# The SSD half of a layer's output projection, emitted between the last GLA heads

## The chip, the cores and the metric

The kernel runs on one core of a Trainium2 chip. The metric is the device time of one execution in microseconds (us). Five engines run side by side, each in the order that its own queue holds: PE (TensorE, matmuls, with PEld for its weight loads), DVE (VectorE), ACT (ScalarE), POOL (GpSimd) and SP (SyncE, which issues most of the weight loads). They wait for each other through semaphores.

## The reference

Two layers of a token mixer with an MLP after each, over 256 latent tokens and 256 context tokens of 1024 channels. The change lies in layer 0. There an SSD scan and a GLA scan (8 heads) run on one input projection, and one output projection takes both halves of their result:

```python
def finish(y, x, z, o, r):
    y = (y + d_skip[:, None] * x).reshape(bn, t, SSD_INNER) * silu(z)
    y = rmsnorm(y.reshape(bn, t, SSD_GROUPS, -1), ...).reshape(bn, t, SSD_INNER)
    o = rmsnorm(o, gla_norm_w).reshape(bn, t, GLA_VAL) * silu(r)
    return concatenate([y, o], axis=-1) @ w_out
...
x = x + g1l * ol          # g1: a gate out of the modulation, silu(c) @ ada_w + ada_b
x = x + g2l * sq_relu_mlp(modulate(rmsnorm(x, norm2_w), sh2l, sc2l), ...)
```

The first 1024 rows of `w_out` meet the SSD half `y`, the other 1024 the GLA half `o`. The gate `g1`, and `sh2`, `sc2`, `g2` for the MLP, come from a matrix product of their own, the modulation.

## The kernel before

Tokens of both kinds make one block of 512. Each fp32 weight tile is loaded by SP into a `wraw` buffer (4 of 512 KB, `RAW`), split by ACT (`whi`) and DVE (`wlo`) into two fp32r parts (`wtile` and `wsplit`, L211 to L225), and each product is three matmuls (`mm3`). An output tile of 128 channels over 1024 input channels is 24 matmuls of 512 columns into one of four PSUM banks called `psd`; small products and transposes go to four banks called `pss`.

The stretch around the change, in the order in which `emit` writes it:

- Left over from the input projection is the SSD gate: `z_proj` (L1242), four groups of two weight tiles and a last step that scales `xtm`, the SSD half with tokens on partitions, by its norm factor (four DVE operations of 128x1024 for `ssqz`). A generator `fill` hands these out; `ZN` says how many steps each turn of the loop takes.
- GLA runs by pairs of heads, t_ = 0 to 3 (called pair 0 to 3 here). `gla_in` (L1268) projects queries and keys (48 matmuls), multiplies the gates (`dlr,gw`), and has for each of the two directions a chain through ACT and DVE (`lin_elem`, L1108: gate, running sum, `ke`, `qt`, `kt`); PE then transposes `ke` and forms the chunk states (`su`, `g0st`, `g1st`). `gla_out` (L1301) makes, for each of the two heads, scores (`qt,kt` matmuls of 64 columns), masks and sums them on DVE (`pm`, `pa`), forms the output on PE (`vtm,pa` and `st,qt`), and normalises it on ACT and DVE into `vtm`. `gla_in` of the next pair is emitted ahead of `gla_out` of this one.
- The modulation is a generator `ad` of two groups (`ada_steps`, L227): each has 8 steps of two raw 512 KB loads and 4 matmuls (line L237; no split), then a copy and 4 transposes. `ADN` says how many steps run in each turn; the first group holds `g1`.
- Then the output projection: for the SSD half (`xtm`) and then the GLA half (`vtm`), 32 transposes turn it to channels on partitions (into `hhi` and `hlo`, or `mgh` and `mgl`), and each of its 8 tiles ends in two gated residual adds on DVE (`add_out`) into the residual stream. The residual stream waits in DRAM (`xd`) and is read back by a 2 MB load that ACT issues as soon as `xtm`, whose space it takes, has been turned.

The order on each engine isn't that of the text: a scheduler of the framework builds the queues from the emitted order, the buffers and its own estimate of times. The queues named below are what it made.

Of the kernel before, what the change touches and what calls it, by code (L numbers as in the profile page):

```python
# [10 lines left out]
F32R = mybir.dt.float32r  # L11
# [3 lines left out]
MUL, ADD, SUB, MIN, MAX = ALU.mult, ALU.add, ALU.subtract, ALU.min, ALU.max  # L15
PSUM = bass.MemoryType.PSUM

P = 128
T = 512
# [10 lines left out]
DTM = 11  # L30
NF = 4
AR = 12
ZN = 3, 1, 2, 2
ADN = 0, 6, 11, 0
WA = 0, 1
QP = -2, 1, 2, 5
VP = -2, -1, 0, -1
GP = -1, 0, 4, 6
# [3 lines left out]
def emit(tc, A, out):  # L42
    nc = tc.nc
    V, S, G, PE, Q = nc.vector, nc.scalar, nc.gpsimd, nc.tensor, nc.sync
    top = ExitStack()

    def pool(name, bufs=1, side=None, stack=top, space=None):
        kw = dict(name=name, bufs=bufs, reuse_waits="tile")
        if side:
            kw["side"] = side  # L50
        if space is not None:
            kw["space"] = space
        return stack.enter_context(tc.tile_pool(**kw))

    cp = pool("const")
    hp = pool("acts")
# [4 lines left out]
    def tl(p, shape, tag, dt=F32, bufs=None):  # L61
        kw = dict(tag=tag, name=tag)
        if bufs is not None:
            kw["bufs"] = bufs
        return p.tile(list(shape), dt, **kw)

    def ps_d():
        return tl(pd, [P, T], "psd")
# [26 lines left out]
    def stt(eng, o, a, s, b, op0, op1):  # L95
        eng.scalar_tensor_tensor(out=o, in0=a, scalar=s, in1=b, op0=op0, op1=op1)  # L96
# [48 lines left out]
    mod = [tl(cp, [P, 48, 2], f"mod{l}") for l in range(2)]  # L145
# [62 lines left out]
    lo_eng = [V]  # L208
    lo_n = [0]

    def wtile(W, k0, kt, c0, n):  # L211

        raw = tl(wp, [P, kt, n], "wraw", bufs=RAW)
        Q.dma_start(out=raw, in_=W[k0 * P:(k0 + kt) * P, c0:c0 + n].rearrange("(k p) c -> p k c", p=P))
        return wsplit(raw, kt, n)
# [44 lines left out]
    def step(it, n=1):  # L260
        for _ in range(n):
            next(it, None)

    def drain(it):
        for _ in it:
            pass
# [8 lines left out]
    HALF = {1: slice(0, 256), 0: slice(256, 512)}  # L275
# [47 lines left out]
    def gemm_f(ps, w, xs, first=True, last=True):  # L323

        n_ = len(xs)
        for k, x in enumerate(xs):
            mm3(ps, (w[0][:, k], w[1][:, k]), x, first and k == 0, last and k == n_ - 1)
# [11 lines left out]
    def ktiles(x, a=slice(None)):  # L339
        return [(x[0][:, k, a], x[1][:, k, a]) for k in range(x[0].shape[1])]  # L340
# [14 lines left out]
    xd = tc.dram_tile([8, P, T], F32, name="xd")  # L355
# [397 lines left out]
    xT = tl(pool("x0", stack=x0, side="right"), [P, 8, T], "xT0")  # L753
# [11 lines left out]
    for k in range(8):  # L765
        ps = ps_s()
# [12 lines left out]
    for k0, nk in ((0, 4), (4, 2), (6, 2)):  # L779
        ps = ps_s()  # L780
        ks, n = slice(k0, k0 + nk), nk * P
# [21 lines left out]
        src = p2[:, :nb * P].rearrange("p (b j h r) -> p j h b r", b=nb, j=2, h=2)[:, :, :, :, 0:2]  # L803
# [11 lines left out]
        for i, m in enumerate(order[:NF]):  # L815
# [3 lines left out]
            for kk in range(k0, k0 + nk):  # L819
                w = [w_[:, kk % 2, c_] for w_ in wq[(kk - k0) // 2]]  # L820
                mm3(first[m], w, (h[0][:, kk], h[1][:, kk]), kk == 0, kk == 7)
        for k in range(k0, k0 + nk):
            ps = ps_s()
# [9 lines left out]
    xp = pool("x", stack=lx)  # L833
    xtm = tl(xp, [P, 4, DM], "xtm")
    lay = ExitStack()
    l0 = pool("l0", stack=lay)
    vtm = tl(l0, [P, 4, DM], "vtm")
# [23 lines left out]
    for m in order:  # L861
        if m in first:
            ps = first[m]
        else:
            w = wtile(W0, 0, 8, 1024 + P * m, P)
            ps = ps_d()
            gemm_f(ps, w, ktiles(h))
        src = tl(cvp, [P, T], "cvs")
# [16 lines left out]
        if m < 4:  # L885
            k = 2 * m
# [47 lines left out]
    ps = ps_s()  # L934
# [5 lines left out]
    ps = ps_s()  # L940
# [109 lines left out]
    scr = [lambda: tl(s2, [P, T], "y", bufs=2)]  # L1050
    adn = [0]
# [6 lines left out]
    ad = counted(ada_all(lambda: scr[0](), (0, 1), (0, 2)))  # L1058
# [15 lines left out]
    fill = v_r_proj()  # L1074
# [157 lines left out]
    gla = ExitStack()  # L1232
# [30 lines left out]
    fill = vr_z()  # L1263

    def gla_w(t_):
        return [wtile(W0, 0, 8, c0 + P * t_, P) for c0 in (3104, 3616)]

    def gla_in(t_, ws):  # L1268
        qk = []
        for w, sc in zip(ws, (0.125, 1.0)):  # L1270
            ps = ps_d()
            gemm_f(ps, w, ktiles(h))
            d_ = tl(g2, [P, T], "gq" if sc != 1.0 else "gk", bufs=QB)
            act(d_, ps, AF.Copy, scale=sc)
            qk.append(d_)

        def chain(d):
            ps = ps_s()
            b0 = 64 + 32 * d
            mm(ps, gw[b0:b0 + 16, t_ * P:(t_ + 1) * P], dlr[b0:b0 + 16])  # L1280
            gb = vB[:, 24 + 4 * d + t_:25 + 4 * d + t_]
            e1 = tl(g2, [P, T], "ge1", bufs=2)
            act(e1, ps, AF.Abs, bias=gb)
            yield
            act(e1, e1, AF.Exp, scale=-1.0)
            yield
            act(e1, e1, AF.Ln, bias=1.0)
            lg = tl(g2, [P, T], "gc", bufs=2)
            ts(V, lg, ps, gb, ADD, 0.0, MIN)
            yield  # L1290
            tt(V, lg, lg, e1, SUB)
            yield
            nm = f"g{d}"
            qt, kt, kd, el, em = yield from lin_elem(g2, d, lg, qk[0], qk[1], None, 1.0 / 16.0, 0, nm)
            sts = yield from lin_states(g2, d, kd, el, em, lambda c, hh: vtm[:, c, (2 * t_ + hh) * P:(2 * t_ + hh + 1) * P],
                                        2, 0, nm)
            return qt, kt, sts

        return both([chain(d) for d in range(2)])

    def gla_out(t_, el_):  # L1301
        for hh in range(2):
            units = []
            r = slice(64 * hh, 64 * hh + 64)
            hd_ = 2 * t_ + hh
            hs_ = slice(hd_ * P, (hd_ + 1) * P)
            for c in range(4):
                cs_ = slice(c * P, (c + 1) * P)
                un = [(r, el_[0][1], el_[0][0], c * P), (r, el_[1][1], el_[1][0], c * P), vtm[:, c, hs_]]
                for d in range(2):  # L1310
                    s_ = el_[d][2].get(c)
                    un.append(None if s_ is None else (el_[d][0][r, cs_], s_[r]))
                units.append(un)

            def put(o, hs_=hs_, hd_=hd_):
                o3 = o.rearrange("p (c f) -> p c f", c=4)
                ov = vtm[:, :, hs_]
                sq = tl(g2, [P, 4, P], "pa", bufs=2)
                for c in range(4):
                    S.activation(out=sq[:, c], in_=o3[:, c], func=AF.Square, accum_out=osq[:, c, hd_:hd_ + 1])  # L1320
                tt(V, ov, o3, sr[:, :, hs_], MUL)
                rstd_small(osq[:, :, hd_:hd_ + 1], 128)
                tt(V, ov, ov, osq[:, :, hd_:hd_ + 1].to_broadcast([P, 4, P]), MUL)

            lin_out(g2, pmask, units, put)

    scr[0] = lambda: tl(g2, [P, T], "ge1", bufs=2)
    cur = gla_in(0, gla_w(0))
    wn = gla_w(1)
    for t_ in range(4):  # L1330
        step(fill, ZN[t_])
        nxt = gla_in(t_ + 1, wn) if t_ < 3 else None
        wn = gla_w(t_ + 2) if t_ < 2 else None
        step(ad, ADN[t_])
        if t_ == 3:
            drain(fill)
            step(ad, max(0, 10 - adn[0]))
        gla_out(t_, cur)
        cur = nxt
    gla.close()  # L1340


    lo_eng[:] = [V]
    WO = A["ssd_gla_w_out"][0]
    mgs = ExitStack()
    mg = pool("mixg", stack=mgs, side="right")
    scr[0] = lambda: tl(mg, [P, T], "adasb")
    for part, src in enumerate((xtm, vtm)):
        if part == 0:
            mx = [tl(hp, [P, 8, T], n, F32R) for n in ("hhi", "hlo")]  # L1350
        else:
            mx = [tl(mg, [P, 8, T], n, F32R) for n in ("mgh", "mgl")]
        for f in range(8):
            ps = ps_s()
            for c in range(4):
                tr(ps[:, c * P:(c + 1) * P], src[:, c, f * P:(f + 1) * P])
            nw = vB[:, 16 + f:17 + f] if part == 0 else vB[:, 96:97]
            act(mx[0][:, f], ps, AF.Copy, scale=nw)
            stt(V, mx[1][:, f], ps, nw, mx[0][:, f], MUL, SUB)
        if part == 0:  # L1360
            xT = tl(xp, [P, 8, T], "xtm")
            S.dma_start(out=xT, in_=xd.rearrange("k p t -> p k t"))
        def add_out(m):
            def put(s, ps):
                a = HALF[s]
                stt(V, xT[:, m, a], ps[:, a], mod[0][:, 16 + m, s:s + 1], xT[:, m, a], MUL, ADD)
            return put

        nf = 8 if part == 0 else 4
        for m in range(nf):  # L1370
            step(ad, WA[part])
            w = wtile(WO, 8 * part, 8, m * P, P)
            ps = ps_d()
            gemm_f(ps, w, ktiles(mx))
            for s in (1, 0):
                add_out(m)(s, ps)
    drain(ad)
    np_ = ExitStack()
    n1 = pool("norm", stack=np_)
# [102 lines left out]
    vtm = tl(l1, [P, 4, DM], "vtm")  # L1482
# [115 lines left out]
    cur = hgrn_in(0)  # L1598
    WO = A["hgrn_s5_w_out"][0]
    for hd_ in range(8):  # L1600
        projs(hd_)
        nxt = hgrn_in(hd_ + 1) if hd_ < 7 else None
# [6 lines left out]
        cur = nxt  # L1609
# [113 lines left out]
```

## Time and profile before

| | us |
|---|---|
| median of 3 runs (lowest, highest) | 1479.78 (1475.62, 1483.78) |
| the profiled execution | 1482.16 |
| its span, first to last instruction | 1480.4 |
| mean granted clock of TensorE in it | 0.973 |

[...] A busy PE isn't PE at its peak. In the chain of work that ended last each step is followed back to what released it. In a timeline row the bracket tells how long the engine sat idle before the row, and for whom.

### The profile page before, as it was taken

The page shows a single profiled execution, that of the slowest core. Times are in us where ns is not written, and L with a number is a line of the kernel's source. Part 1 is how long each engine was busy: PE and PEld are TensorE (multiplying, and loading weights), DVE is VectorE, ACT ScalarE, POOL GpSimd, SP SyncE. Part 2 cuts the span into 40 slices and gives each one's busy share as a digit, 9 for nine tenths or more (in the row PEclk, how much of TensorE's full clock was granted, in tenths as well). Part 3 has the DMA queues.
Part 4 walks back from the last instruction along what each step waited for, and adds up shares of the span by engine and source line. Part 5 has one row for each costly group of instructions (what it writes and reads, how often), then busy time and mean ns, then how long its engine had stood idle before and what let it go on. Part 6 is the DMA issues. An engine that isn't in the chain of part 4 may idle for free.

```text
span 1480.4 us, 24457 instructions
## 1 busy us (share of the span) xinstructions
PE 1426.6 (96%) x9662; PEld 1222.3 (83%) x9662; DVE 942.2 (64%) x1596; ACT 688.3 (46%) x1316; POOL 303.0 (20%) x340
## 2 busy tenths in 40 slices
PE   6999999999979999999999999999999999899998
PEld 4788998878746889877777777799988888899998
DVE  4698678876753455854563743374886988655543
ACT  5565545375532234531322422353286786555532
POOL 3000000000000003098077861122500000044210
PEclk9999999999985999999999999999999999999999
DMA  9733444421275433466467656649835332566762
GB/s 333 185 92 85 126 122 118 125 58 58 86 240 160 138 103 105 121 179 197 143 187 218 192 169 186 192 165 202 194 114 157 103 106 66 157 186 170 206 179 86
DMA packets 291151, 222.45 MB, mean 150 GB/s; under 512 B 22902, under 2 KB 270124, under 8 KB 291036
## 3 DMA queue, kind: packets, MB, share of 16 engines
q1 hardware_dynamic: 252752, 182.75, 42.5%
q0 software_dynamic: 6144, 22.05, 4.9%
q10 hardware_dynamic: 32140, 16.09, 4.4%
q8 instruction: 76, 1.25, 0.4%
q14 instruction: 39, 0.32, 0.1%
HBM read 206.39 MB, written 14.46 MB: 149 GB/s over the span
## 4 chain that ended last, share of the span: by engine, by line
PE 78%; DVE 8%; DMA 8%; ACT 4%; issue 2%; ACTq 0%; SPq 0%; DVEq 0%
PE psd L99 65%; PE pss L99 6%; DMA R<-acd 3%; PE pss L237 3%; PE pss L107 2%; DMA araw<-in_ada_w_dram 2%; DVE wlo L87 1%; DMA wraw<-in_ada_w_dram 1%; ACT hL L80 1%; DVE xtm L87 1%; ACT whi L80 1%; PE pss L652 1%; DMA U<-ud 0%; DMA ud<-s5r 0%; ACT R L80 0%
## 5 line engine op out<-in xcount | busy, mean ns | idle before, releaser
L87 DVE TENSOR_TENSOR wlo<-wraw,whi 128x1024 fp32r<-128x1024 f32 (+1 forms) x250 | 323.6, 1298 | 206.7 <-ACT whi L80 205.0
L80 ACT ACTIVATE whi<-wraw 128x1024 fp32r<-128x1024 f32 (+1 forms) x250 | 260.6, 1045 | 351.7 <-DMA wraw<-in_mlp_w_dram 170.7
L99 PE MATMUL psd<-hlo,whi 128*128 128x512 f32 (+1 forms) x1112 | 381.6, 345 | 1.3 <-DVE hlo L87 1.3
L99 PE MATMUL psd<-hhi,whi 128*128 128x512 f32 (+1 forms) x1112 | 378.5, 348 | 3.6 <-ACT hhi L80 3.6
L99 PE MATMUL psd<-hhi,wlo 128*128 128x512 f32 (+1 forms) x1112 | 380.8, 344 | 0.6 <-DVE wlo L87 0.6
L99 PEld LDWEIGHTS psd<-hhi,whi 128*128 128x128 f32 x1112 | 209.5, 191 | 36.0 <-ACT hhi L80 4.2
L99 PEld LDWEIGHTS psd<-hlo,whi 128*128 128x128 f32 x1112 | 211.3, 190 | 25.2 <-DVE hlo L87 2.3
L99 PEld LDWEIGHTS psd<-hhi,wlo 128*128 128x128 f32 x1112 | 211.3, 190 | 25.1 <-DVE wlo L87 1.0
L99 PE MATMUL psd<-wlo,hhi 128*128 128x256 f32 x576 | 165.5, 288 | 2.8 <-DVE wlo L87 2.8
L99 PE MATMUL psd<-whi,hlo 128*128 128x256 f32 x576 | 164.8, 286 | 0.0
L99 PE MATMUL psd<-whi,hhi 128*128 128x256 f32 x576 | 164.4, 287 | 0.0
L99 PEld LDWEIGHTS psd<-wlo,hhi 128*128 128x128 f32 x576 | 111.1, 193 | 4.7 <-DVE wlo L87 3.0
L99 PEld LDWEIGHTS psd<-whi,hhi 128*128 128x128 f32 x576 | 110.8, 193 | 2.7 <-issue 1.3
L99 PEld LDWEIGHTS psd<-whi,hlo 128*128 128x128 f32 x576 | 111.1, 193 | 0.6 <-issue 0.2
L99 PE MATMUL psd<-hidh,whi 128*128 128x512 f32 (+1 forms) x288 | 107.7, 375 | 0.0
L99 PE MATMUL psd<-hidl,whi 128*128 128x512 f32 (+1 forms) x288 | 105.6, 367 | 0.0
L99 PE MATMUL psd<-hidh,wlo 128*128 128x512 f32 (+1 forms) x288 | 105.5, 366 | 0.0
L87 POOL TENSOR_TENSOR nsa<-nsa,nsq 128x256 f32<-128x256 f32 x28 | 26.1, 934 | 370.1 <-ACT nsq L80 369.8
L96 DVE SCALAR_TENSOR_TENSOR xtm<-psd,mod,xtm 128x256 f32<-128x256 f32 x96 | 42.2, 476 | 66.6 <-PE psd L99 59.2
L99 PE MATMUL psd<-hl,whi 128*128 128x256 f32 x256 | 72.9, 285 | 0.0
L99 PE MATMUL psd<-hh,wlo 128*128 128x256 f32 x256 | 72.9, 285 | 0.0
L99 PE MATMUL psd<-hh,whi 128*128 128x256 f32 x256 | 72.4, 283 | 0.0
(448 smaller groups left out, 2447.4 us busy)
## 6 DMA issues: line engine op xcount, KB each, us to landing
wraw<-in_mlp_w_dram SPq DMA_DIRECT2D x128, 512.0 KB, 4.2
wraw<-in_ada_w_dram SPq DMA_DIRECT2D x80, 512.0 KB, 3.8
wraw<-in_ssd_gla_w_in_dram SPq DMA_DIRECT2D x48, 512.0 KB, 4.2
wraw<-in_hgrn_s_w_in_dram SPq DMA_DIRECT2D x43, 512.0 KB, 4.2
araw<-in_ada_w_dram SPq DMA_DIRECT2D x32, 256.0 KB, 7.8
R<-acd ACTq DMA_DIRECT2D x32, 256.0 KB, 3.9
wraw<-in_ssd_gla_w_out_dram SPq DMA_DIRECT2D x16, 512.0 KB, 4.6
wraw<-in_hgrn_s_w_out_dram SPq DMA_DIRECT2D x12, 384.0 KB, 3.4
```

The source lines that it names most:

```text
L80: ins = S.activation(out=out_, in_=in_, func=func, scale=scale, bias=bias)
L87: eng.tensor_tensor(out=o, in0=a, in1=b, op=op)
L96: eng.scalar_tensor_tensor(out=o, in0=a, scalar=s, in1=b, op0=op0, op1=op1)
L99: PE.matmul(o, lhsT=l, rhs=r, start=start, stop=stop, skip_group_check=True)
L107: PE.transpose(o, i, ident[:rows, :rows])
L237: ins = PE.matmul(ps[32 * gg:32 * gg + 32], lhsT=cs[:, k], rhs=raws[gg // 2][:, gg % 2 * T:gg % 2 * T + T], start=(k == 0), stop=(k == 7), ...
L652: PE.matmul(ps[64 * t2:64 * t2 + 64, 64 * a:64 * a + 64], lhsT=W1[i][:, a0 + a, 64 * t2:64 * t2 + 64], rhs=U[:, 2 * (a0 + a) + t2], start= ...
```

## The change

The SSD half of the output projection becomes a generator `ssd_out` that is emitted inside the loop over pairs: its 32 turns and 4 tiles behind the heads of pair 2, the other 4 tiles behind those of pair 3 (`SN`). One step of the modulation goes beside each of its 8 tiles (`step(ad)`), where before 17 steps ran in the loop's turns 1 and 2 (`ADN` 0, 6, 11, 0) and the last three beside the GLA half. Gate groups of `z_proj` go one turn later (`ZN` 3, 1, 2, 2 becomes 2, 1, 1, 1), and the rest of `fill` is drained in turn 2, not 3. The GLA half stays behind the loop.

```diff
-ZN = 3, 1, 2, 2
-ADN = 0, 6, 11, 0
-WA = 0, 1
+ZN = 2, 1, 1, 1
+ADN = 0, 6, 4, 0
+SN = 0, 0, 5, 4
...
+    def out_tile(mx, part, m):
+        w = wtile(WO, 8 * part, 8, m * P, P)
+        ps = ps_d()
+        gemm_f(ps, w, ktiles(mx))
+        for s in (1, 0):
+            add_out(m)(s, ps)
+
+    def ssd_out():
+        mx = [tl(hp, [P, 8, T], n, F32R) for n in ("hhi", "hlo")]
+        turned_mix(mx, xtm, 0)
+        res["x"] = tl(xp, [P, 8, T], "xtm")
+        S.dma_start(out=res["x"], in_=xd.rearrange("k p t -> p k t"))
+        yield
+        for m in range(8):
+            step(ad)
+            out_tile(mx, 0, m)
+            yield
...
+    so = ssd_out()
     for t_ in range(4):
         step(fill, ZN[t_])
         nxt = gla_in(t_ + 1, wn) if t_ < 3 else None
         wn = gla_w(t_ + 2) if t_ < 2 else None
         step(ad, ADN[t_])
-        if t_ == 3:
+        if t_ == 2:
             drain(fill)
-            step(ad, max(0, 10 - adn[0]))
+            step(ad, 10 - adn[0])
         gla_out(t_, cur)
+        step(so, SN[t_])
         cur = nxt
```

What the scheduler makes of it, at three places. First PE, where the keys of pair 2 are transposed (`ident,ke`), behind the gates of that pair (`dlr,gw`). Before, the gates of pair 2 are followed by 48 projection matmuls (`psd`):

```order
L99 MATMUL psd<-hhi,wlo 128x512
L99 MATMUL pss<-dlr,gw 128x512 x2
L99 MATMUL psd<-hhi,whi 128x512
L99 MATMUL psd<-hlo,whi 128x512
...
L99 MATMUL psd<-hhi,wlo 128x512
L107 MATMUL pss<-ident,ke 128x128 x6
L99 MATMUL pss<-vtm,g0kd 64x128 x2
```

After, the same gates stand inside the output of the heads of pair 0:

```order
L99 MATMUL pss<-vtm,pa 128x128
L99 MATMUL pss<-dlr,gw 128x512 x2
L99 MATMUL pss<-vtm,pa 128x128
L99 MATMUL pss<-g0st_3058,g0qt 128x128
L99 MATMUL pss<-vtm,pa 128x128
L99 MATMUL pss<-g0st_3072,g0qt 128x128
L99 MATMUL pss<-g1st_3093,g1qt 128x128
L99 MATMUL pss<-vtm,pa 128x128
L99 MATMUL pss<-g0st_3086,g0qt 128x128
L99 MATMUL pss<-g1st_3079,g1qt 128x128
L99 MATMUL pss<-vtm,pa 128x128
L107 MATMUL pss<-ident,ke 128x128 x6
```

Between gates and keys there are now nine small matmuls, the output of one head, in place of 48 projection matmuls.

Second DVE, where `xtm` is scaled (`xtm,ssqz`). Before, this stands ahead of the chain of pair 2 (`gc` is its gate), while PE has projection matmuls:

```order
L87 TENSOR_TENSOR vtm<-pss,sr 128x4x128
L87 TENSOR_TENSOR xtm<-xtm,ssqz 128x1024 x3
L87 TENSOR_TENSOR vtm<-vtm,osq 128x4x128
L87 TENSOR_TENSOR xtm<-xtm,ssqz 128x1024
L93 TENSOR_SCALAR gc<-pss,vB 128x512 x2
```

After, it stands behind the chain of pair 3 and ahead of that pair's states (`su`) and the masks (`pm`) of the heads of pair 2:

```order
L87 TENSOR_TENSOR ke<-ke,gk 128x384
L87 TENSOR_TENSOR ke<-ke,gk 128x512
L87 TENSOR_TENSOR g0kt<-gk,g0kt 128x512
L87 TENSOR_TENSOR g1kt<-gk,g1kt 128x512
L87 TENSOR_TENSOR xtm<-xtm,ssqz 128x1024 x4
L96 SCALAR_TENSOR_TENSOR su<-su,el,pss 128x128
L87 TENSOR_TENSOR wlo<-wraw,whi 128x1024
L96 SCALAR_TENSOR_TENSOR su<-su,el,pss 128x128
L87 TENSOR_TENSOR mod_88<-pss,vA 128x16 x2
L96 SCALAR_TENSOR_TENSOR su<-su,el,pss 128x128 x2
L1192 COPY_PREDICATED pm_2917<-mf,pss 64x512
```

The states, the modulation's bias add and the masks have moved behind the four scalings. Third DVE, at the heads of pair 3. Before, their masks follow those of pair 2, with no residual add between:

```order
L1196 COPY_PREDICATED pm_2918<-mb,pss 64x512
L87 TENSOR_TENSOR pa<-pm_2917,pm_2918 128x512
L87 TENSOR_TENSOR vtm<-pss,sr 128x4x128
L87 TENSOR_TENSOR vtm<-vtm,osq 128x4x128
L1192 COPY_PREDICATED pm_2917<-mf,pss 64x512
```

After, the residual adds of the first SSD tile (`xtm<-psd,mod,xtm`, which need the 2 MB load) stand ahead of the masked sum `pa` of pair 3's first head:

```order
L1196 COPY_PREDICATED pm_2918<-mb,pss 64x512
L96 SCALAR_TENSOR_TENSOR xtm<-psd,mod_88,xtm 128x256 x2
L87 TENSOR_TENSOR pa<-pm_2917,pm_2918 128x512
L1192 COPY_PREDICATED pm_2917<-mf,pss 64x512
L1193 COPY_PREDICATED pm_2917<-mf,pss 64x4x64
L1195 COPY_PREDICATED pm_2918<-mb,pss 64x4x64
L1196 COPY_PREDICATED pm_2918<-mb,pss 64x512
L87 TENSOR_TENSOR wlo<-wraw,whi 128x1024
L87 TENSOR_TENSOR pa<-pm_2917,pm_2918 128x512
```

That load and the split of the second SSD tile (`wlo`) are now on the way of pair 3's heads. On SP, 30 modulation loads in a row and then 8 of `w_out` have become 12, two of the last gate group, 6, and from there one `w_out` load and two modulation loads by turns.

## Rows read from the trace of the kernel before

**Rows 1.** The page, parts 1 and 4: busy time by engine; shares of the chain.

```profile
PE 1426.6 (96%) x9662; PEld 1222.3 (83%) x9662; DVE 942.2 (64%) x1596; ACT 688.3 (46%) x1316; POOL 303.0 (20%) x340
...
PE 78%; DVE 8%; DMA 8%; ACT 4%; issue 2%; ACTq 0%; SPq 0%; DVEq 0%
```

**Rows 2.** Windows: stretch, length, busy us (PE, PEld, DVE, ACT, POOL), PEclk, DMA share, GB/s.

```profile
396.00:423.00 27.00, 22.15 (x191) 12.24 (x191) 18.42 (x32) 12.70 (x42) 0.00 (x0) 1.00 0.64 214
423.00:441.00 18.00, 13.02 (x124) 6.16 (x116) 9.96 (x19) 5.97 (x16) 0.00 (x0) 0.80 0.77 262
441.00:488.00 47.00, 47.00 (x209) 30.97 (x206) 17.86 (x25) 11.31 (x45) 0.00 (x0) 0.50 0.52 158
```

**Rows 3.** Waits of PE from 285 to 565 us: total, times, longest.

```profile
PE pss L237 <- DMA wraw<-in_ada_w_dram: 8.2, 5, 3.2
PE psd L99 <- DVE wlo L87: 2.8, 1, 2.8
```

**Rows 4.** Timeline of PE, pair 1: start, us, operation; scores, output, modulation step.

```profile
406.01 1.09 PE L99 MATMUL pss<-g1qt,g1kt 64*64 64x64 f32 x16
407.03 0.49 PE L99 MATMUL pss<-vtm,pa 128*128 128x128 f32 x2
...
410.81 1.06 PE L237 MATMUL pss<-wraw,cs 128*32 128x512 f32 x8
```

**Rows 5.** Timeline of PE, pair 2: the same three; then the first SSD tile.

```profile
441.28 1.97 PE L99 MATMUL pss<-g1qt,g1kt 64*64 64x64 f32 x16
443.19 0.79 PE L99 MATMUL pss<-vtm,pa 128*128 128x128 f32 x2
...
449.83 1.93 PE L237 MATMUL pss<-wraw,cs 128*32 128x512 f32 x8
...
484.84 2.05 PE L99 MATMUL psd<-hhi,whi 128*128 128x512 f32 x4
```

**Rows 6.** Timeline of PE: pair 2's gates, first projection matmul, keys; a modulation step.

```profile
383.47 1.13 PE L99 MATMUL pss<-dlr,gw 16*128 16x512 f32 x4
384.53 0.50 PE L99 MATMUL psd<-hhi,whi 128*128 128x512 f32 x1
...
395.55 0.49 PE L107 MATMUL pss<-ident,ke 128*128 128x128 f32 x3
...
422.53 1.06 PE L237 MATMUL pss<-wraw,cs 128*32 128x512 f32 x8 [3.20 <-DMA wraw<-in_ada_w_dram]
```

**Rows 7.** Timeline of DVE: first step of pair 2's chain, last of each direction's keys.

```profile
386.82 1.40 DVE L93 TENSOR_SCALAR gc<-pss,vB 128x512 f32<-128x512 f32 x2
...
393.85 0.55 DVE L87 TENSOR_TENSOR ke<-ke,gk 128x384 f32<-128x384 f32 x1
...
395.52 0.68 DVE L87 TENSOR_TENSOR ke<-ke,gk 128x512 f32<-128x512 f32 x1
```

**Rows 8.** Groups of DVE from 380 to 490 us: count, busy us, mean ns, idle before.

```profile
L87 DVE TENSOR_TENSOR vtm<-pss,sr 128x512 f32<-128x512 f32 x7 | 4.8, 691 | 8.3 <-ACT pa L1320 8.2
L87 DVE TENSOR_TENSOR wlo<-wraw,whi 128x1024 fp32r<-128x1024 f32 x4 | 4.8, 1221 | 0.2 <-ACT whi L80 0.2
...
L87 DVE TENSOR_TENSOR xtm<-xtm,ssqz 128x1024 f32<-128x1024 f32 x4 | 4.7, 1217 | 0.0
```

**Rows 9.** DMA issues: count, KB each, median us from issue to landing.

```profile
wraw<-in_ada_w_dram SPq DMA_DIRECT2D x80, 512.0 KB, 3.8
...
xtm<-xd ACTq DMA_DIRECT2D x1, 2048.0 KB, 8.9
```

**Rows 10.** Windows, as in rows 2, where the clock came back.

```profile
428.00:430.00 2.00, 2.00 (x11) 0.80 (x7) 0.17 (x1) 1.31 (x3) 0.00 (x0) 0.50 0.34 72
430.00:432.00 2.00, 1.30 (x23) 1.08 (x21) 1.47 (x3) 1.94 (x7) 0.00 (x0) 0.92 0.95 334
...
486.00:488.00 2.00, 2.00 (x10) 1.70 (x9) 0.69 (x1) 0.88 (x6) 0.00 (x0) 0.50 0.02 6
488.00:490.00 2.00, 2.00 (x11) 1.70 (x10) 1.50 (x3) 1.26 (x3) 0.00 (x0) 0.91 0.00 0
```

More of the change, by code (lines that the diff above doesn't have):

```diff
@@ L1327, in emit, with turned_mix @@
     scr[0] = lambda: tl(g2, [P, T], "ge1", bufs=2)
[L1328 to L1334, printed above, removed]
-        if t_ == 3:
-            drain(fill)
-            step(ad, max(0, 10 - adn[0]))
[L1338 to L1343, printed above, removed]
-    WO = A["ssd_gla_w_out"][0]
[L1345 to L1352, printed above, removed]
+    WO = A["ssd_gla_w_out"][0]
+    res = {}
+    def turned_mix(mx, src, part):
         for f in range(8):
@@ L1359, in emit, with add_out, put @@
             stt(V, mx[1][:, f], ps, nw, mx[0][:, f], MUL, SUB)
[L1360 to L1376, printed above, removed]
+    def add_out(m):
+        def put(s, ps):
+            a = HALF[s]
+            x_ = res["x"][:, m, a]
+            stt(V, x_, ps[:, a], mod[0][:, 16 + m, s:s + 1], x_, MUL, ADD)
+        return put
+    def out_tile(mx, part, m):
[14 more added lines that the diff above has]
+            yield
+    cur = gla_in(0, gla_w(0))
+    wn = gla_w(1)
+    so = ssd_out()
+    for t_ in range(4):
+        step(fill, ZN[t_])
+        nxt = gla_in(t_ + 1, wn) if t_ < 3 else None
+        wn = gla_w(t_ + 2) if t_ < 2 else None
+        step(ad, ADN[t_])
+        if t_ == 2:
+            drain(fill)
+            step(ad, 10 - adn[0])
+        gla_out(t_, cur)
+        step(so, SN[t_])
+        cur = nxt
+    gla.close()
+    lo_eng[:] = [V]
+    mgs = ExitStack()
+    mg = pool("mixg", stack=mgs, side="right")
+    scr[0] = lambda: tl(mg, [P, T], "adasb")
+    mx = [tl(mg, [P, 8, T], n, F32R) for n in ("mgh", "mgl")]
+    turned_mix(mx, vtm, 1)
+    xT = res["x"]
+    for m in range(4):
+        step(ad)
+        out_tile(mx, 1, m)
     drain(ad)
```

## The prediction

> **What bounds the kernel now.** I read the page first: PE is busy for 1426.6 of 1480.4 us, 96%, and has 78% of the chain of work that ended last [rows 1]. The change neither adds nor removes a product. All it can move is what PE loses, and that is read where the change lies, from about 300 us to the end of the projection at about 561. The second view is windows of that stretch [rows 2]: from 441 to 488 us PE is busy for 47.00 of 47 us at a clock of 0.50, and from 423 to 441 the mean is 0.80. So there is a loss that no busy share shows. The third view is the waits of PE [rows 3]: 8.2 us for modulation weights, 2.8 for one split weight tile.
>
> The price of the half clock comes from the timeline, the same three operations in pair 1 and in pair 2: scores of one direction 1.09 and 1.97 us, the output of one head 3.78 and 6.64, a modulation step 1.06 and 1.93 [rows 4, 5]. That is 1.8 times. Of 47 us at half clock, 47 x (1 - 1/1.8) = 20.9 are lost. A mean of 0.80 over 18 us is 7.2 us at half; 13.02 of 18 are busy, so 5.2, of which 2.3 are lost. Before, PE loses **11.0 + 20.9 + 2.3 = 34.2 us** here. The smaller waits for ACT and masks I take as unchanged.
>
> **The change part by part.** The question is what PE loses after; every term is an estimate from rows.
>
> *Wait for the split tile.* The gate groups of `z_proj` go one turn later, and the queue of PE has projection matmuls of pair 1 where it had to wait. The 2.8 us go. Loss after: 0.
>
> *Keys of pair 2.* This is the first new wait. Before, 48 projection matmuls (384.53 to 395.55) stand between the gates of pair 2 and its keys, and cover the chain on DVE: PE then waits for next to nothing [rows 6]. After, nine small matmuls stand there, 3.6 us by the output of a head (3.78 less its overlap [rows 4]). From the end of the gates, the chain takes 386.82 to 394.40 = 7.6 us to its first `ke` and 1.8 more to the second (396.20) [rows 7]; gates and chain before had 2.2 us between them (384.60 to 386.82), for ACT. DVE also has three operations on `vtm` of 0.69 [rows 8] for the heads of pair 0 in its queue, 2.1. So the first `ke` comes 7.6 + 2.2 + 2.1 = 11.9 us behind the gates, against 3.6 of work on PE: some 8.1 of wait, and 0.9 before the second. I take **9**. Below: some of the 2.1 and 2.2 overlap, 5. Above: ACT does its part behind other work, 11. Queued behind the keys on PE are the states of pair 2, two modulation steps and the heads of pair 1, so nothing hides this.
>
> *Clock behind that wait.* Before, the clock fell behind a wait of 3.20 us [rows 6]; it was at 0.50 in 428:430 and at 0.92 in 430:432, after modulation steps and transposes of keys [rows 10]. A wait of 9 us will bring it down too, and keys, states and two modulation steps run at half. If it comes back as there, half of some 6.5 us of work is at stake: **3** (2 to 5).
>
> *Modulation weights.* Of 20 steps, six run in turn 1 and four in turn 2; the last eight go one by one beside the SSD tiles, with some 6 us of PE work for three loads of 512 KB, where a load lands 3.8 us after its issue [rows 9]. The 8.2 us were waits of steps that stood close together [rows 3]. I leave 0.3 for them and 0.4 for the last gate group's weights: **0.7** (0 to 4, half of what it was).
>
> *States of pair 3 and masks of pair 2 behind `xtm`'s scaling.* The second new wait. Behind the key projection of pair 3, DVE has the two `ke` (0.55 + 0.68 [rows 7]), two `kt` at the same 0.68, four scalings of 1.217, 4.7 in all [rows 8], and only then the first `su`, about 0.5, which frees the first of the four `pss` banks. That is 7.8 us. PE has two modulation steps, 2.1 [rows 4], keys 1.1 and the state products and transposes some 1.7: 4.9. So 3 us of wait, and 1 more, since the `wlo` between the first two `su` takes 1.22 [rows 8]. **4** (2 to 6).
>
> *Clock in pair 2's heads.* Waits of 3.20 and less, in small work, brought the clock down before [rows 3, 6], and 47 us of work of this kind, without a wait, didn't bring it back [rows 2, 5]. After, scores of two heads (4 x 1.09 + 0.2 = 4.6), the two outputs (3.6 + 3.4) and some of the 32 turns (1.0), 12.6 us, come before projection matmuls. At 1.83 times, that is 10.4. When the first SSD tile came, from 484.84 on, the clock was back within 488:490 [rows 5, 10], so four more us at half, two of them lost, and 0.4 for turns among them: **12.8**. This takes the place of the 20.9, and the heads of pair 3, which were in that stretch, now have projection matmuls between them.
>
> [...] In the trace PE was busy for 47.00 of 47 us at 0.50 [rows 2]. [...]
>
> *The residual stream.* ACT issues the 2 MB load when the last turn of `xtm` is done, some 6.3 us behind pair 2's last output; it lands 8.9 us later [rows 9], at 15.2. The first residual adds stand on DVE ahead of `pa` of pair 3's first head. PE reaches that head's output at about 15.4, and two adds and `pa`, 0.95 and 0.7, make that 17.1 instead. With 0.5 for the later `wlo` and `pa`: **2.3**. Above: 2 MB beside 2 MB of SP's loads at the 262 GB/s of the second window [rows 2] is 16 us for both, not 8.9, so 6 more; 1 to 8.
>
> [...]
>
> *`w_out` between modulation weights.* SP now has one `w_out` load and two modulation loads by turns; some tile may be late. **1** (0 to 3).
>
> **The sum.** 0 + 9 + 3 + 0.7 + 4 + 12.8 + 2.3 + 1 = 32.8, against 34.2: -1.4 us. The profiled execution took 1482.16, so 1480.8; it lies 2.4 above the median of 1479.78, so **1478**. DVE, ACT and POOL keep the same instructions, and the GLA half behind the loop stays.
>
> **The rivals.**
>
> *Slower: the half clock stays through the heads of pair 1.* Behind the wait at pair 2's keys there is small work alone: scores of two heads 4.4, outputs 7.2, four further modulation steps 4.2, two gates 2.2 [rows 4, 6], 18.0 us, and only then projection matmuls. If the clock isn't back before them, 18.0 x 0.83 = 14.9 and 1.5 until the projection brings it back: +16.4, **1495**. For it: 441 to 488 [rows 2]. Against it: the return by 430:432 in the same kind of work [rows 10]. It decides from the point where the clock is still at half when pair 1's scores begin.
>
> *Faster: pair 2's heads run at full clock.* If the wait behind the scalings is short, or the 28 projection matmuls just ahead of it keep the clock up, the 12.8 go: **1466**. For it: 396 to 423, with waits in it and a clock of 1.00 [rows 2]. Against it: rows 5. [...]
>
> *Both:* half in pair 1, full in pair 2: 1478.4 + 16.4 - 12.8 = 1482, within the forecast. That the change doesn't do what it says is excluded by the queues.
>
> **How the numbers follow.** I give 0.58 to a return before pair 1's heads, and 0.68 to half clock in pair 2's. Forecast 0.58 x 0.68 + 0.42 x 0.32 = 0.53, with a range of its own of 1471 to 1487, the terms' bounds taken as independent; slower rival 0.42 x 0.68 = 0.28; faster one 0.19. The range goes to 1463 and 1497: outside lie two fifths of each rival, 0.19. 0.5%, about what a measurement here can tell from no change, is 7.4 us: 1472.4 and 1487.2. Faster: most of the faster rival, 0.16, and a quarter of the forecast, 0.13. Slower: 0.23 of the slower rival, and 0.07 of the forecast. That leaves 0.41 for the same.
>
> **What would show it.** Windows of 2 us over PE give the clock: I expect 0.50 behind the keys of pair 2, 1.00 in pair 1's heads, 0.50 in pair 2's, 1.00 from the SSD tiles on. In the waits of PE: `ke` on DVE with some 8 us at pair 2's keys; `su` with 3 to 4; in those of DVE, the load of `xtm` with 1 to 3; modulation weights below 1. A clock at half in pair 1's scores makes the slower rival, one at full in pair 2's the faster. The forecast is wrong as a whole if the wait at pair 2's keys is under 4 us, or if a wait that I haven't named is over 5.

## The result, and the profile after

The changed kernel ("after" from here on) takes 1490.68 us, median of 8 runs (1482.96 to 1502.07), the kernel before 1477.36 beside it (1460.64 to 1483.78): ratio 1.0124, 95% interval 1.0078 to 1.0169, **slower by some 13 us**. Ratios leave disturbed runs out, so they can differ a little from the quotient of the medians.

The profiled execution of after took 1502.07 us, the longest of the 8; a second one (experiment e10) took 1492.59. Both are read below. First the page, parts 1 and 4, of the first profile:

```profile
PE 1443.5 (96%) x9662; PEld 1231.6 (82%) x9662; DVE 943.0 (63%) x1596; ACT 687.3 (46%) x1316; POOL 303.6 (20%) x340
...
PE 75%; DMA 10%; DVE 4%; issue 4%; POOL 4%; ACT 2%; SPq 1%; ACTq 0%; POOLq 0%; DVEq 0%
```

PE has the same 9662 matmuls as in [rows 1], but is busy 16.9 us longer, and still 96% of its span. So most of what came is no wait: the same matmuls took longer. The windows from the first gates of pair 0 to the first matmul of the MLP (columns as in [rows 2]; PEclk is the granted clock of TensorE, 1.00 its highest value in the trace) hold most of the difference, before first, then after:

```profile
297.05:560.89 263.84, 251.18 (x1512) 191.01 (x1512) 153.25 (x232) 116.74 (x295) 2.90 (x2) 0.89 0.39 121
```

```profile
297.10:576.20 279.10, 263.76 (x1511) 197.18 (x1511) 153.79 (x232) 116.26 (x295) 2.87 (x2) 0.84 0.37 115
```

This stretch got 15.3 us longer: 2.7 of them idle, 12.6 busy, at a mean clock of 0.84 instead of 0.89. The other 4.6 us of the 19.9 between the two spans lie outside it, where both kernels do the same work: by the account below 24.7 us are busy at half clock there in after and 14.9 in before, 4.4 us of loss. Where the clock was lost, window by window in after:

```profile
358.00:364.00 6.00, 5.98 (x80) 4.85 (x77) 4.79 (x9) 0.85 (x2) 0.00 (x0) 1.00 0.00 0
366.00:374.00 8.00, 8.00 (x24) 4.85 (x22) 6.06 (x9) 4.77 (x16) 0.00 (x0) 0.50 0.00 0
380.00:384.00 4.00, 3.10 (x21) 2.04 (x21) 2.43 (x6) 2.06 (x6) 0.00 (x0) 0.50 0.01 4
386.00:390.00 4.00, 3.50 (x50) 1.99 (x42) 1.53 (x3) 0.22 (x1) 0.00 (x0) 1.00 0.61 174
394.00:418.00 24.00, 24.00 (x87) 12.39 (x84) 10.67 (x15) 7.30 (x26) 0.00 (x0) 0.50 0.39 129
454.00:476.00 22.00, 22.00 (x109) 17.92 (x107) 9.78 (x16) 4.81 (x23) 0.00 (x0) 0.50 0.04 15
494.00:500.00 6.00, 6.00 (x21) 4.28 (x20) 2.98 (x4) 1.97 (x9) 0.00 (x0) 0.50 0.40 118
```

In order: the scores of pair 0 at full clock; its outputs at half; the keys of pair 2 at half; the first scores of pair 1 at full; the rest of pair 1's heads, pair 2's heads, and an output of pair 3's heads, at half. In before it was 441 to 488 and some us around 423 to 430 [rows 2, 10]. The waits of PE in the stretch (as [rows 3]), and where the fourth row ends, in the timeline of PE:

```profile
PE pss L107 <- DVE ke L87: 6.2, 2, 5.3
PE pss L107 <- DVE su L96: 3.1, 1, 3.1
PE pss L237 <- DMA wraw<-in_ada_w_dram: 2.2, 1, 2.2
PE pss L99 <- DVE su L96: 2.2, 1, 2.2
PE pss L99 <- DVE pa L87: 0.7, 1, 0.7
```

```profile
389.01 0.48 PE L99 MATMUL pss<-g1st,g1qt 64*128 64x128 f32 x2
391.70 1.06 PE L237 MATMUL pss<-wraw,cs 128*32 128x512 f32 x8 [2.20 <-DMA wraw<-in_ada_w_dram]
```

The 8.2 us for modulation weights and the 2.8 for a split tile [rows 3] became 2.2 and none; 6.2 for `ke` and 5.3 for `su` came.

**An account of the stretch.** For each profile the stretch was cut into windows of 1 us. A busy us at 0.50 counts as one us at half clock, one at 0.75 as half of one: in windows of 1 us over its whole span, before shows 1.00 in 1391, 0.50 in 74, and something between in the 15 that hold a change (after 1369, 109 and 22); each us at half clock costs 1 - 1/1.8 = 0.444 us, the price of [rows 4, 5]. What is left after idle time and this loss is the work at full clock:

| kernel | stretch | PE idle | busy at half | lost by it | rest | median, all runs | ratio to before (95%) |
|---|---|---|---|---|---|---|---|
| before | 263.8 | 12.6 | 55.6 | 24.7 | 226.5 | 1477 to 1482 | |
| after, first profile | 279.1 | 15.3 | 80.6 | 35.8 | 228.0 | 1490.7 | 1.0124 (1.0078 to 1.0169) |
| after, second (e10) | 272.7 | 16.9 | 61.1 | 27.2 | 228.7 | 1492.9 | 1.0118 (1.0051 to 1.0185) |
| e1 old gates | 264.1 | 16.0 | 43.5 | 19.3 | 228.8 | 1482.2 | 1.0047 (1.0001 to 1.0094) |
| e2 old place | 285.4 | 22.3 | 77.2 | 34.3 | 228.9 | 1504.1 | 1.0147 (1.0121 to 1.0172) |
| e3 dense in pair 1 | 280.2 | 16.2 | 64.8 | 28.8 | 235.2 | 1496.5 | 1.0085 (1.0034 to 1.0136) |
| e4 turns ahead | 258.4 | 14.8 | 30.2 | 13.4 | 230.1 | 1474.3 | 0.9966 (0.9914 to 1.0018) |
| e5 no scaling | 263.8 | 14.1 | 47.8 | 21.2 | 228.5 | 1486.2 | 1.0072 (1.0024 to 1.0120) |
| e6 fewer loads | 272.2 | 19.1 | 57.8 | 25.7 | 227.5 | 1478.5 | 1.0023 (0.9978 to 1.0069) |
| e7 turns before chain | 263.2 | 17.3 | 33.4 | 14.8 | 231.1 | 1475.1 | 0.9995 (0.9951 to 1.0038) |
| e8 steps early | 268.7 | 17.4 | 43.6 | 19.3 | 232.0 | 1485.5 | 1.0078 (1.0039 to 1.0117) |
| e9 dense in pair 0 | 267.8 | 17.4 | 33.2 | 14.7 | 235.7 | 1490.9 | 1.0111 (1.0044 to 1.0178) |
| e11 steps late | 250.7 | 15.3 | 12.5 | 5.6 | 229.8 | 1470.5 | 0.9979 (0.9934 to 1.0023) |
| e12 both late | 272.7 | 22.2 | 46.0 | 20.4 | 230.1 | 1492.1 | 1.0111 (1.0047 to 1.0175) |

The rest is 226 to 232 us in every kernel, and 235 to 236 in the two that have 6 to 7 us of matmuls more. So idle time and half clock make up nearly all of the stretch's differences: of the 15.3 us of the first profile, 11.1 are half clock, 2.7 waits and 1.5 unexplained; of the 8.9 of the second, 2.5, 4.3 and 2.2. One profile is one draw: the clock's share changes from execution to execution (80.6 and 61.1 us at half in the same kernel), and verdicts rest on all runs.

Every run also has a mean granted clock on record, which gives an estimate without a profile: 2 x (1 - clock) x span is the time at half clock, and 0.444 of it is lost if PE is busy in all of it. By it, e10's four runs lose 41.0 us in the mean and the 17 runs of before beside them 31.3: 9.7 us of the 15.0 that lie between their mean times. What is left, 5.3, is of the size of the waits and the unexplained part in e10's profile (6.5).

### The profile page after: what moved, and what is told of

It is laid out like the page before. It is cut to its first block, busy times and chain, and to the rows that moved or that the text cites. A ratio compares the mean times of both kernels' runs of the same rounds, so it can differ in the third digit from the quotient of the medians.

```text
span 1500.3 us, 24438 instructions
## 1 busy us (share of the span) xinstructions
PE 1443.5 (96%) x9662; PEld 1231.6 (82%) x9662; DVE 943.0 (63%) x1596; ACT 687.3 (46%) x1316; POOL 303.6 (20%) x340
## 4 chain that ended last, share of the span: by engine, by line
PE 75%; DMA 10%; DVE 4%; issue 4%; POOL 4%; ACT 2%; SPq 1%; ACTq 0%; POOLq 0%; DVEq 0%
PE psd L99 60%; PE pss L99 9%; PE pss L107 2%; DMA araw<-in_ada_w_dram 2%; DMA R<-acd 2%; PE pss L237 2%; DMA wraw<-in_ssd_gla_w_out_dram 1%; DVE wlo L87 1%; POOL cmb L87 1%; POOL cma L87 1%; DMA wraw<-in_mlp_w_dram 1%; POOL ph L87 1%; ACT whi L80 1%; DMA xtm<-xd 1%; DMA wraw<-in_ssd_gla_w_in_dram 1%
## 5 line engine op out<-in xcount | busy, mean ns | idle before, releaser
L99 PE MATMUL psd<-hhi,whi 128*128 128x512 f32 (+1 forms) x1112 | 382.7, 350 | 4.6 <-ACT hhi L80 3.6
```

Source lines behind the costliest of these rows:

```text
L99: PE.matmul(o, lhsT=l, rhs=r, start=start, stop=stop, skip_group_check=True)
```

## The experiments

Two theories: **clock**, after is slower since its heads have become stretches of small matmuls that run at half clock; and **waits**, the new waits of PE cost, and the half clock is their sign. Beside them stood the question which part of the change does it, the tables (`ZN`, `ADN`) or the split of the SSD half (`SN`). "The stretch" is the one above.

**e1, the gate groups back.** `-ZN = 2, 1, 1, 1` / `+ZN = 3, 1, 2, 2`.

> The gate groups of z_proj go back to the turns of the kernel before (ZN 3, 1, 2, 2); the split of the output projection stays. Clock theory (after is slower because its heads of pairs 0, 1 and 2 are stretches of small matmuls with no projection matmuls among them, and run at a clock of 0.50): pair 0's heads and pair 2's keys are covered again, the wait of 6.2 us for ke and the waits of 5.3 us for su go, pair 3's heads keep the SSD tiles; half clock only in pair 2's heads. 1466 to 1474, faster than before by 3 to 12 us. Rival, the split itself costs (residual load, w_out beside modulation weights, residual adds on DVE): 1485 to 1492, as after.

1482.2 us, the stretch as before's: 264.1. The waits of PE for `ke` and `su` on DVE went, and pair 0's half clock with them (every us from 331 to 388 is at 1.00); 6.5 us for modulation weights, 3.7 for a split tile and 2.0 for `su` on ACT, ahead of pair 2's heads, stand in their place. The time did not come down to the forecast of 1466 to 1474, as the half clock wasn't in pair 2's heads alone:

```profile
434.00:456.00 22.00, 22.00 (x117) 17.89 (x117) 9.54 (x19) 4.59 (x20) 0.00 (x0) 0.50 0.09 25
474.00:482.00 8.00, 8.00 (x28) 5.50 (x27) 5.54 (x8) 2.81 (x12) 0.00 (x0) 0.50 0.52 148
```

The first is pair 2's heads, the second an output of pair 3. So the split without the moved gate groups gains nothing and costs 0 to 14 us by its interval; moving the gate groups made most of the loss.

**e2, the split undone.** `-SN = 0, 0, 5, 4` / `+SN = 0, 0, 0, 9`.

> The new tables for gate groups and modulation stay, but the whole SSD half is emitted behind the last heads (SN 0, 0, 0, 9). Clock theory: the waits at pair 2's keys and the half clock in pair 1's heads are there as in after, and pair 3's heads have no projection matmuls among them: 1490 to 1500, no better than after. Rival, the split itself costs: 1475 to 1480, as before.

1504.1 us, even above the range: the new tables alone cost more than the whole change. Pair 1's heads, and pair 2's and 3's in one piece, are at half:

```profile
390.00:414.00 24.00, 24.00 (x86) 12.31 (x84) 10.60 (x15) 7.44 (x27) 0.00 (x0) 0.50 0.39 129
450.00:480.00 30.00, 30.00 (x168) 23.34 (x165) 13.79 (x23) 3.30 (x20) 0.00 (x0) 0.50 0.03 11
```

In the account, this kernel's stretch loses to half clock what after's first profile loses (34.3 and 35.8 us) and 7.1 more than the second; PE sits idle 7.0 and 5.4 us longer. Among its waits are some behind the heads that after has not, or has smaller:

```profile
PE pss L107 <- DVE mgl L96: 3.0, 2, 2.3
PE psd L99 <- ACT whi L80: 2.7, 4, 1.2
PE psd L99 <- DVE wlo L87: 2.1, 4, 0.5
```

So with the new tables the split gains some 13 us, 5 to 7 of them in waits.

**e3, dense matmuls behind pair 2's keys.** After, and:

```
+    def dense(n, el_):
+        ps = ps_d()
+        for k in range(n):
+            mm(ps, el_[1][1][:, 0:P], el_[1][0], k == 0, k == n - 1)
...
+        if t_ == 1:
+            dense(8, nxt)
```

> After, with eight more matmuls of 128x512 in fp32 on full tiles, whose result nothing uses, among the states of pair 2, behind the wait for its keys. At full clock they are worth about 7 us, at half 13. Clock theory: they bring the clock back, the scores of one direction in pair 1 take 1.09 us and not 1.7 to 2.0, some 12 us of half clock go, and the time is that of after within 6 us although there is more to do. Rival, the waits alone cost and the half clock is their sign: the scores stay at half, and the time is that of after plus 8 to 14 us.

1496.5 us, 5.8 above the median of after: just inside the 6 of the clock theory, but the half clock that was to go is still there. The windows behind the added matmuls, and the row where the full clock ends:

```profile
382.00:392.00 10.00, 9.97 (x82) 5.08 (x80) 2.64 (x7) 2.25 (x6) 0.00 (x0) 1.00 0.20 51
396.00:422.00 26.00, 24.85 (x89) 13.08 (x86) 9.77 (x14) 8.60 (x30) 0.00 (x0) 0.50 0.41 128
```

```profile
394.41 1.64 PE L237 MATMUL pss<-wraw,cs 128*32 128x512 f32 x8 [1.14 <-DMA wraw<-in_ada_w_dram]
```

The clock was up for the first scores, as it was in after, and fell at the same place, at the first modulation step in the midst of pair 1's scores. Eight dense matmuls ahead of the heads didn't hold the clock through them. The fall came behind a wait again, of 1.14 us, so this run doesn't tell whether the wait or the small matmuls brought it.

**e4, turns and tiles ahead of the heads.** As e1 (with `ZN` 3, 1, 1, 1; up to the heads of pair 2 the trace has e1's order of matmuls), and:

```
+PRE = 0, 0, 2, 2
-SN = 0, 0, 5, 4
+SN = 0, 0, 3, 2
...
+        step(so, PRE[t_])
         gla_out(t_, cur)
```

> As e1, and the 32 turns with the first SSD tile are emitted ahead of pair 2's heads, one tile ahead of pair 3's: projection matmuls then stand between the keys of pair 3 and the heads of pair 2, and among the heads of pairs 2 and 3. Clock theory: pair 2's and pair 3's heads at 0.9 to 1.00, 8 to 12 us less than e1, 1455 to 1464. Rival (waits): the heads wait longer for masks and residual adds that now come first on DVE, the time is that of e1 or more.

1474.3 us, 7.9 less than e1 beside it, though not down to the 1455 to 1464 of the forecast; the stretch is 5.7 us shorter, half clock 13 us less. (By `PRE` two tiles go ahead of pair 3's heads, not one, as the entry says.) The first half of what was to be at full clock is, the second isn't:

```profile
444.00:456.00 12.00, 11.82 (x96) 7.12 (x95) 4.85 (x8) 2.09 (x4) 0.00 (x0) 1.00 0.68 213
458.00:472.00 14.00, 14.00 (x54) 9.02 (x53) 7.96 (x12) 3.08 (x12) 0.00 (x0) 0.50 0.41 116
```

The second window is an output and scores of pair 2 with two projection matmuls and one modulation step among them. The clock fell at 456.7, behind dense work, and no wait before it was over 0.2 us.

**e5, no scaling of `xtm`.** After, without the four DVE operations (`xtm<-xtm,ssqz`).

> After, without the four scalings of xtm on DVE (left out, 4.9 us of DVE work; the queue of PE stays as it is). It takes away the two waits of PE for su, 5.3 us, ahead of pair 2's heads, and nothing else. If a wait is what brings the clock down there: pair 2's heads stay at 1.00, and 5 + 11 us go, 1472 to 1477. If small matmuls alone bring it down, as in pair 0's heads of after, where PE had no wait: the clock falls some us into pair 2's heads, 5 to 10 us go, 1480 to 1486. If neither counts (the wait is made up later): 1488 to 1492.

1486.2 us: some 5 less than after, the upper end of the middle case. The waits for `su` went, and pair 2's scores ran at full clock (1.00 to 443 us); but then PE waited for the masks (`pm`), and the clock fell behind that wait:

```profile
PE pss L99 <- DVE pm L1196: 2.6, 1, 2.6
```

So taking a wait away gave that wait, less the next one, and of the clock only the scores. That the outputs would have fallen without the new wait isn't shown. (In this profile the clock also came back in the middle of pair 1's heads, at 399 us; the medians are what to go by.)

**e6, fewer modulation loads.** After; six of eight steps of the first group reuse the two raw tiles of the step before.

> After, with six of the first eight modulation steps taking the weights of the step before (12 of 16 loads of 512 KB left out, all matmuls kept). The weights of the next gate group then come earlier, and its projection matmuls stand among the heads of pair 1, where after has none. Clock theory: pair 1's heads at 0.9 to 1.00 and not 0.50, 11 us and the wait of 2.2 us go, the stretch to the MLP is 13 us shorter, 1476 to 1480. Rival (waits): 2 us go, 1487 to 1490.

1478.5 us, as the clock theory had it: with projection matmuls among pair 1's heads, half clock there is 396 to 403 us instead of 392 to 419, and begins with no wait over 0.2 us near. The profiled execution took 1489.4, 11 above the median. Of its stretch only 6.9 us went, not 13, as pair 3's gates now stand right ahead of its keys, with two modulation steps between, and wait for `ke` like pair 2's:

```profile
PE pss L107 <- DVE ke L87: 15.7, 4, 7.2
```

**e7 and e8, modulation steps earlier.** Both from e4 with `ADN` 2, 4, 4, 0; e7 also emits the turns and two tiles (`PRE` 3; not three, as its entry says) between pair 3's projection and its gates.

> As e4, with modulation steps 2, 4, 4 in turns 0 to 2, and the turns with three SSD tiles emitted between pair 3's projection and its gates. Projection matmuls then stand among the heads of pairs 0 and 2, under the keys of pairs 2 and 3 and around the modulation steps; only pair 1's heads are small work alone, behind 48 projection matmuls. Clock theory: half clock in pair 1's heads at most, the stretch 6 to 10 us shorter than in e4, 1462 to 1469. Rival (DVE and ACT can't keep up with turns, splits and chains that now fall together): waits take what the clock gives, 1473 or more.

> As e4, with modulation steps 2, 4, 4 in turns 0 to 2, so that they stand among projection matmuls; the gates of pair 3 have only small work behind them, and its keys wait some 5 us as pair 2's do in after. Clock theory: the waits for modulation weights (6.6 us in e4) go, the wait for ke comes, and behind it the turns bring the clock back: within 4 us of e4, 1470 to 1477. Rival (waits for weights are what e4 still loses): 5 us below e4 or more, under 1469.

e7 1475.1 us, e8 1485.5: neither beats e4's 1474.3. The waits of PE in e7, then in e8:

```profile
PE psd L100 <- ACT whi L81: 6.2, 2, 3.9
PE pss L238 <- DMA wraw<-in_ada_w_dram: 5.0, 3, 3.4
```

```profile
PE pss L109 <- DVE ke L89: 8.1, 3, 6.4
```

In e7 the modulation steps beside the tiles fell together with pair 3's keys and waited for their weights, with ACT's splits late as well: the rival of that entry held. e8 came out above both of its forecasts: the small work behind pair 3's gates is too short to cover its chain, and the wait for `ke` (8.1 us in all) with half clock around it (43.6 us in the stretch, 30.2 in e4) costs more than the weights had.

**e9, dense matmuls among pair 0's heads.** After; 24 matmuls of `hhi` by `hhi`, emitted ahead of pair 1's modulation steps.

> After, with 24 more matmuls of 128x512 (fp32r, as the projection's), whose result nothing uses, emitted ahead of pair 1's modulation steps; the scheduler puts them among pair 0's scores, gates and outputs. There PE had no wait in after, and the clock fell to 0.50 all the same. At full clock they are worth 5.6 us, and those behind the gates lie under the wait for ke. If small matmuls alone bring the clock down there: it stays at 1.00 through pair 0's heads, 4 to 5 us of half clock go, the wait for ke gets 2 to 3 us shorter, and the time is that of after within 4 us although there are 5.6 us more to do. If something else brings it down (the gates, the state of the chip): 0.50 there again, and 3 to 6 us more than after.

1490.9 us, 2 less than after beside it, with 5.6 us of matmuls more. Pair 0's heads, then pair 1's, and the wait for `ke`:

```profile
360.00:378.00 18.00, 18.00 (x123) 12.71 (x119) 12.75 (x23) 6.18 (x20) 0.00 (x0) 1.00 0.00 1
...
396.00:408.00 12.00, 12.00 (x71) 6.72 (x71) 6.92 (x10) 5.60 (x26) 0.00 (x0) 1.00 0.59 185
```

```profile
PE pss L107 <- DVE ke L87: 5.2, 1, 5.2
```

With dense matmuls among them pair 0's heads run at full clock to their end; in after, without a wait, they had fallen. That is the clock theory's plainest case, and worth 4 us in the first profile of after, about 1 in the second. The wait got 1 us shorter, not 2 to 3, since the heads ahead of it got faster. That pair 1's heads stayed at full clock too was not expected. The profiled execution, 1491.3, is a usual one of e9's four: its stretch is 4.9 us shorter than e10's, and the rest of its span 3.6 us longer; by the estimate from the mean clocks (0.978 and 0.971) some 28 us of that rest are at half clock, against some 15 in e10.

Pair 1's heads in e9 have no dense matmul from 375 us on, as after's have none. One thing that differs is the wait at their first modulation step, here and in e10:

```profile
394.49 1.07 PE L237 MATMUL pss<-wraw,cs 128*32 128x512 f32 x8 [0.99 <-DMA wraw<-in_ada_w_dram]
```

```profile
388.49 1.79 PE L237 MATMUL pss<-wraw,cs 128*32 128x512 f32 x8 [2.29 <-DMA wraw<-in_ada_w_dram]
```

Over the profiles that have this wait: behind 2.20 and 2.29 (after), 2.54 (e2), 1.14 (e3) and 2.85 us (e5) the clock fell within about 1 us, and behind 1.01 (before), 1.05 (e1), 0.97 (e4) and 0.99 (e9, e11) it held to the end of the heads. So in pair 1's heads the wait, as the waits theory has it, is not excluded as what starts the half clock. No run changes that wait alone.

**e10, after once more.**

> After once more, unchanged, beside the others, for a second profile. Clock theory: the places of 0.50 come again in the heads of pairs 0, 1 and 2, and the stretch from pair 0's gates to the MLP is over 270 us; 1486 to 1494. If the first profile was of a chance: half clock lies elsewhere, and the stretch is within 5 us of the kernel before's 263.8.

The same places: pair 1's, pair 2's and pair 3's heads, and the keys of pair 2; of pair 0's heads only the end. The time is in the forecast.

```profile
358.00:366.00 8.00, 7.97 (x78) 5.71 (x74) 6.05 (x10) 1.10 (x9) 0.00 (x0) 1.00 0.00 0
...
390.00:418.00 28.00, 28.00 (x109) 15.71 (x106) 11.86 (x17) 9.79 (x33) 0.00 (x0) 0.50 0.41 126
448.00:466.00 18.00, 16.09 (x97) 13.23 (x98) 8.29 (x16) 3.65 (x14) 0.00 (x0) 0.50 0.13 43
```

**e11 and e12, modulation steps late.** From e4 and from e7: `step(ad, 1 if m >= 4 else 0)` in place of `step(ad)` beside the SSD tiles.

> As e4, with the modulation's steps beside the last four SSD tiles and the GLA tiles alone, not beside all eight SSD tiles. SP then loads w_out without modulation weights between, and more projection matmuls stand among the heads of pairs 2 and 3. Clock theory: the half clock of e4 in pair 2's heads (457 to 473 us there) goes, 7 us, 1464 to 1470. Rival (residual load and adds on DVE hold these heads, not the clock): as e4, 1472 to 1478.

> As e7, with the modulation's steps late as in e11. In e7 PE waited for modulation weights at pair 3's keys and the clock fell behind them (438 to 450 and 460 to 484 us). Clock theory: 5 to 8 us less than e7, 1466 to 1471. Rival: the waits move on to w_out, as e7, 1473 to 1477.

e11 takes 1470.5 us, just above the clock theory's range (12 runs, 11 of them 1466.9 to 1475.2), its stretch 13.1 us less than before's. Pair 1's heads, with no projection matmul in them and 48 ahead of pair 2's keys, have no fall; pair 2's and 3's heads have none either, with turns and projection matmuls among them:

```profile
396.00:416.00 20.00, 18.76 (x156) 10.35 (x148) 12.34 (x20) 7.30 (x29) 0.00 (x0) 1.00 0.66 217
446.00:512.00 66.00, 66.00 (x398) 47.95 (x396) 27.92 (x45) 10.26 (x35) 0.00 (x0) 1.00 0.39 127
```

It is clear of after (four runs of 1487.4 to 1497.1 beside it). Of before it isn't: 1481.1 in the median there, but 4 of its 17 runs lie at 1462 to 1466, and the interval of the ratio holds 1. These short runs have a mean clock of 0.985 to 0.988, the other 13 one of 0.970 to 0.975; by the estimate above that is 19 us, and the two groups lie 18 us apart. So the clock accounts for the gap. In which heads it held was not seen: none was profiled.

e12 takes 1492.1, outside both of its forecasts and as slow as after: the keys of pair 3 wait, and the clock is at 0.50 from 450 to 460 us, in the end of that wait and behind it. In e12 only 1.2 us of projection matmuls stand between the gates of pair 3 and its keys; in e7 a wait of 3.9 us for `whi`, more projection matmuls and a modulation step stood there and covered that chain: PE came to these keys at 452.07 us without a wait.

```profile
PE pss L108 <- DVE ke L88: 10.9, 3, 8.7
```

## Why the prediction was wrong

It forecast 1478, no change that can be measured; 1490.7 was measured, inside the range but on the slower side, which had 0.30. By its own steps (first profile; the losses at half clock are busy us times 0.444):

- **Wait for the split tile**: gone, as forecast.
- **Keys of pair 2**: 9 forecast, 5 to 11; 6.2 measured, 7.4 in the second profile. Right.
- **Clock behind that wait**: 3 forecast; 379.5 to 385.8 us, 5.4 us busy, so 2.4. Right, and the return before pair 1's scores came as forecast (386 to 390 at 1.00).
- **Modulation weights**: 0.7; 2.2, within the bounds, but right ahead of the fall in pair 1's heads.
- **States behind the scaling**: 4; 5.3. Right.
- **Clock in pair 2's heads**: 12.8; 452.4 to 477.5 us, 25.1 us busy, so 11.1. Right: from 454 to 476 us PE was busy for 22.00 of 22 us at 0.50. The faster rival fell.
- **Residual stream**: 2.3; 0.7 for `pa`. The upper end didn't come: DVE sat idle for 0.4 us until that load.
- **`w_out`**: 1; 0.

What the sum didn't have:

- **Pair 1's heads: the step that failed.** The prediction asked only whether the clock is back when pair 1's scores begin, and took it to last from there, from the one stretch of 396 to 423 [rows 2]. It came back and fell again at 392.6, behind a wait of 2.2 us for modulation weights, to 418.2: 25.6 us busy, 11.4 lost, where the slower rival had 14.9; in the second profile the same, 28.00 us in 390 to 418. So the rival's price held roughly and its point of decision was wrong. The prediction itself wrote that waits of 3.20 us and less had brought the clock down in small work; it allowed the modulation weights a wait of up to 4 us and priced no clock behind it.
- **Pair 0's heads**: 365.6 to 374.2, 8.6 us busy, 3.8 lost. The prediction looked for the clock behind waits alone. Here there was none: the gate groups that moved a turn later had stood among these heads, and what was left was small. The same cause was seen in the order of PE, and read only as the loss of a cover for the keys. In the second profile this was 1 to 2 us at half before the wait.
- **Pair 3's heads**: 491.8 to 500.5, 8.5 us busy, 3.8 lost, in the output of the first head, behind dense work and the wait of 0.7 for `pa`.

These three are 19.0 us; the rest of the sum came out 5 below the forecast's 32.8, at 27.9. The chance of 0.58 on "the clock returns before pair 1's heads" was put on the wrong event: the return came, and the loss too. The queue of PE after has no projection matmul from pair 0's scores to the end of pair 1's heads, and this could be read ahead of the run. That it alone brings the clock down in pair 1's heads isn't shown: in e9 and e11 those heads have none either and ran at 1.00. That the time lies near the slower rival's 1495 is in part luck, as pair 0's and pair 3's heads were not in that sum.

## What to carry to other kernels

When projection matmuls are moved out from among small matmuls, price the stretch that they leave at half clock too, even if PE will wait for nothing there: in after PE was busy for 8.00 of 8 us at 0.50 (366 to 374) and for 22.00 of 22 (454 to 476). The busy share didn't show it, the granted clock by windows did. Heads with dense matmuls among them ran at 1.00 to their end in e9 (pair 0, 360 to 378) and e11 (446 to 512); eight ahead of the heads did not hold it (e3, 0.50 from 396 to 422), while 48 ahead of pair 2's keys stood before heads that held it (before, 396 to 423; e11, 396 to 416). A wait that stands just ahead of small matmuls may cost more than its length: 2.2 us stood ahead of 11.4 lost, and which of the two brought the clock down stays open. And read several profiles, or all runs, before one term is believed: two executions of the same kernel had 80.6 and 61.1 us at half clock in this stretch.

## What the runs showed of the hardware that was not expected

The clock fell from 1.00 to 0.50 with PE busy for 5.98 of 6 and then 8.00 of 8 us (after, 358 to 374), in scores of 64 rows, outputs of 128 columns and the gates of pair 2, and stayed at 1.00 through the same heads with 24 matmuls of 512 columns among them (e9, 360 to 378, busy for 18.00 of 18). In between, nearly the same sequence of small matmuls did both: in e11 pair 1's heads ran 20 us at 1.00, busy for 18.76; in e10 28 us at 0.50, busy for 28.00. Ahead of them stood 48 projection matmuls in e11 and none in e10, and the wait at the first modulation step was 0.99 us in e11 and 2.29 in e10; e9, with none just ahead and 0.99, held. What decides in a given execution stays open.
